# Gated delta rule in one fused decoder layer: the second gate of a unit is projected behind the unit's values

## Chip, cores and metric

The kernel runs on one core of a Trainium2 chip. The metric is device time in microseconds, the median over runs. The engines in the profile are PE (TensorE matmuls; PEld its weight loads), DVE (VectorE), ACT (ScalarE), POOL (GpSimd) and SP (SyncE, which issues DMAs).

## What is computed

One layer of a hybrid decoder on 2048 tokens of width 1024. One input projection feeds four head groups (retention, gated delta rule, S5, GLA), each gated by a SiLU gate; an output projection maps their concatenation back. The change touches the gated delta rule group (4 heads, chunks of 64 tokens):

```python
def _deltanet_branch(qkv, beta_in, a_in, gate, ...):
    qkv = silu(_causal_conv(qkv, conv_w))            # 4 taps, per channel
    q, k, v = split and reshape to heads
    o = _gated_delta_rule(q, k, v, sigmoid(beta_in), g)
    return _merge(_head_rmsnorm(o, norm_g)) * silu(gate)

def _gated_delta_rule(q, k, v, beta, g):             # per chunk of 64
    a_mat = strictly lower part of (kb @ k.T) * decay
    u, w  = solve (I + a_mat) with right sides v*beta and kb*exp(gcum)
    # over the chunks, in order:
    v_new = u - w @ state
    o     = qg @ state + attn @ v_new
    state = state * gl + kg.T @ v_new
```

## The kernel before

The projections are matmuls in split fp16: 24 matmuls of 128x256 (8 slices of the contraction, 3 products of high and low parts) give one 128x256 block. `proj_ops` (line 301 in the trace) projects a tile of 128 tokens, `projT_ops` (line 309) gives 128 channels of a unit of 256 tokens, transposed.

The delta rule is the phase `phase_dn`. It works on 8 units of 256 tokens (two tiles, t = 0 and 1) in a software pipeline: step s of the loop projects and convolves unit s (`conv`), prepares unit s - 1 (`dn_front`, `dn_sub`), and finishes unit s - 2 (`dn_back`). The pieces are:

- `conv(s)`: the dense stream. Keys (dk), queries (dq) and values (dv), two halves of 128 channels each: 24 matmuls of line 309, then ScalarE copies the block out of PSUM (raw, line 1473) and makes the first tap (cva, line 1478), VectorE adds three taps (cva), ScalarE takes a tanh (cvt, line 1484) and VectorE the last product (ckq or cv, line 1488). Between the matmuls `conv` calls `dn_pre` five times: GpSimd builds masked decays (dgx, line 1557), TensorE sums them (line 1568, once per tile), ScalarE exponentiates (dE), GpSimd multiplies by masks (dmb, line 1570); then ScalarE squares keys and queries (dsq, line 1575), TensorE adds up the squares (line 1582), and VectorE makes the norms (depsq, dkk, dry, drt and so on) and scales dmb.
- `dn_front` multiplies keys with keys and queries (line 1627) and scales by dmb. `dn_sub` solves the 16x16 diagonal blocks on VectorE (28 small products dgm and dsV), with the data laid out through DRAM by SyncE's DMAs.
- `dn_back` joins the blocks (lines 1734 to 1776, with the additions dT of line 1755 and copies on ScalarE), forms u and w (lines 1786, 1787), and runs the state through the four chunks. For each chunk TensorE multiplies w with the state (line 1812), VectorE subtracts (VS, line 1813), TensorE makes the next state (line 1818) out of the decays dKG, which GpSimd builds (lines 1804, 1805), and ScalarE copies it (VS, line 1820). Line 1824 gives the outputs of a tile. `finish` squares them (fsq), makes a reciprocal square root on VectorE (fss, fry, frt, frr) and multiplies by the gate.
- The gate of a tile (`gate_ops`): 24 matmuls of line 301, a tanh on ScalarE (th, line 371), and a product on VectorE (dgg, line 375).

`emit` interleaves the streams in proportion: the dense stream, 17 places for `dn_back`, 9 for `dn_front`. Work for other engines is put off by a number of places (`later`, `string`). The order in which an engine gets its instructions then comes from a scheduler of the framework, and each engine works strictly in that order. In steps s = 2 to 7 the dense stream holds both gates of unit s - 2 besides the projections of unit s:

```python
gate = [list(self.gate_ops(..., 2 * u + t, "dgg", ...)) for t in range(2)]
g0, g1 = (0, 104)
dense = dense[:g0] + gate[0] + dense[g0:g1] + gate[1] + dense[g1:]
```

`dense` has 161 places, 52 for the keys, 54 for the queries, 55 for the values; place 104 is the last matmul of the queries' second half. All blocks of these projections share two PSUM buffers (`psA`, tile name pa).

Of the kernel before, what the change touches and what calls it, by code (L numbers as in the profile page):

```python
# [155 lines left out]
class Trunk:  # L156
# [1262 lines left out]
    def phase_dn(self):  # L1419
# [5 lines left out]
        P = self.dP = self.pool("dn", bufs=2, side="right")  # L1425
# [16 lines left out]
        kq, vv, fr, tt, gates = {}, {}, {}, {}, {}  # L1442
# [55 lines left out]
        def sg_ops(i):  # L1498
            return self.gate_ops(P, *self.W["sg"], i, "cva", lambda x: nc.sync.dma_start(self.y[i * 128:(i + 1) * 128, 512:768], x), P1)

        def loads(s, j):
            a, b = {(NU, 0): (1, 0), (NU, 1): (2, 1), (NU, 2): (3, 2), (NU, 3): (0, 3)}.get((s, j), (0, 0))
            ops = [lambda: self.load_b(f"wo{b}")] if b else []
            return ops + [lambda: self.load_a(f"wo{a}")] if a else ops

        def steps(gen, n):

            return [lambda: next(gen, None)] * n

        for s in range(NU + 2):  # L1510
            streams = []
            dense = list(conv(s)) if s < NU else []
            u = s - 2
            if u >= 0:
                gate = [list(self.gate_ops(P, *self.W["dg"], 2 * u + t, "dgg", lambda g, t=t: gates.__setitem__(2 * u + t, g))) for t in range(2)]
                if s < NU:
                    g0, g1 = (0, 104)
                    dense = dense[:g0] + gate[0] + dense[g0:g1] + gate[1] + dense[g1:]
                else:
                    sg = [op for i in (range(10) if s == NU else range(10, NT)) for op in sg_ops(i)]  # L1520
                    n = len(sg) // 3
                    sg = loads(s, 0) + sg[:n] + loads(s, 1) + sg[n:2 * n] + loads(s, 2) + sg[2 * n:] + loads(s, 3)
                    tg = int(len(sg) * 0.717)
                    dense = gate[0] + sg[:tg] + gate[1] + sg[tg:]
                state = [VS]
                streams.append(steps(self.dn_back(u, fr.pop(u), tt.pop(u), state, gates), 16) + [lambda: None])
            u1 = s - 1
            if 0 <= u1 < NU:
                streams.append(steps(self.dn_front(u1, kq[u1], vv[u1], fr[u1], tt), 4) + [lambda: None] * 5)
            if s == NU + 1:  # L1530
                self.out_open()
                self.fronts = {}
                streams.append([op for i in range(2) for op in steps(self.out_front(i, self.out_room[i].__getitem__, self.fronts), 3)])
            self.emit(dense, *streams)
            if u >= 0:
                VS = state[0]
            if s in (3, 5):
                self.load_a("sg" if s == 3 else "wo0")
            if s in (4, 6):
                self.load_b("sg" if s == 4 else "wo0")  # L1540
# [441 lines left out]
```

## Time and profile before

| | us |
|---|---|
| median of 3 runs | 1224.54 (1223.58 to 1227.66) |
| the profiled execution | 1231.87 |
| its span | 1229.8 |
| PE busy in the span | 1116.9 (91%) |
| DVE busy | 911.0 (74%) |
| ACT busy | 505.7 (41%) |
| POOL busy | 471.1 (38%) |
| mean granted TensorE clock | 0.959 |

Durations of single instructions come from the one profiled execution, whose span is the time between its first and last instruction. A row of the trace's timeline gives the start, the length, engine, line, operation and tiles (output <- inputs), and in brackets the idle time of the engine just before and what ended it. Lines with a count group instructions that follow each other.

The steps s = 2 to 7 start at about 658, 706, 752, 801, 846 and 896 us, by the tanh of their first gate, and the last of them hands over about 942 us. Steps 4 and 6 (752 and 846 us) also carry the preparation of one more weight matrix (`load_b`, lines 262 to 265).

### The profile page before, as it was taken

Reading aid. Unit: us, or ns where it says so; the run is one execution under the profiler, and the core shown is the slowest. Engines: PE = TensorE matmul, PEld = TensorE weight load, DVE = VectorE, ACT = ScalarE, POOL = GpSimd, SP = SyncE. Lnnn points to the kernel's source line nnn. Section 1 sums busy time; section 2 is a strip of 40 time slices with the busy share of each in tenths; the row PEclk is TensorE's granted clock in tenths of the full one; section 3 lists DMA queues with packets and bytes.
Section 4 is the critical chain, followed back from the end, with each engine's and each line's share of the span. In section 5 each row is a group of like instructions: output and inputs, shape, how many; then the busy total and the mean of one; then the engine's idle time right before and its main releaser. Section 6 shows DMA issues by size and latency. Waiting matters only on the chain. (4 is left out here: it accounts for less than half of the span.)

```text
span 1229.8 us, 38305 instructions
## 1 busy us (share of the span) xinstructions
PE 1116.9 (91%) x15687; PEld 929.8 (76%) x15687; DVE 911.0 (74%) x3237; ACT 505.7 (41%) x1124; POOL 471.1 (38%) x848
## 2 busy tenths in 40 slices
PE   3889999999999999989779889898899999899996
PEld 2767788888878887877667677677777877788885
DVE  6779655445888788887797877877787744778885
ACT  5733322124444444453454344344443533443431
POOL 3112111111676666563552432533522312444433
PEclk9899999999989999999998998999899989999999
DMA  8565611201121111221212121211123616567652
GB/s 288 146 168 129 173 62 35 70 31 57 26 61 36 36 35 36 65 61 23 88 46 34 28 42 18 61 27 34 30 58 81 181 44 194 140 187 177 183 138 86
DMA packets 186911, 104.97 MB, mean 85 GB/s; under 512 B 158000, under 2 KB 173552, under 8 KB 184560
## 3 DMA queue, kind: packets, MB, share of 16 engines
q1 hardware_dynamic: 186160, 102.00, 32.1%
q8 instruction: 123, 2.02, 0.7%
q10 hardware_dynamic: 576, 0.52, 0.1%
q14 instruction: 52, 0.43, 0.1%
HBM read 59.43 MB, written 26.23 MB: 70 GB/s over the span
## 5 line engine op out<-in xcount | busy, mean ns | idle before, releaser
L301 PEld LDWEIGHTS <-xT 128*128 128x128 f16 x3456 | 337.4, 101 | 78.3 <-issue 22.0
L301 PE MATMUL pa<-w,xT 128*128 128x256 f16 x3072 | 384.4, 280 | 7.4 <-DVE w L265 3.3
L309 PE MATMUL pa<-xT,w 128*128 128x256 f16 x1536 | 202.4, 281 | 8.8 <-ACT raw L1473 7.0
L309 PEld LDWEIGHTS <-w 128*128 128x128 f16 x1536 | 147.7, 101 | 35.6 <-issue 11.1
L1858 PE MATMUL o<-w,yT 128*128 128x256 f16 x1344 | 155.5, 276 | 7.4 <-DMA yT<-y 7.3
L1858 PEld LDWEIGHTS <-yT 128*128 128x128 f16 x1344 | 132.5, 99 | 27.9 <-DMA yT<-y 10.0
L153 DVE SCALAR_TENSOR_TENSOR cva<-raw,cw,cva 128x256 f32<-128x256 f32 x144 | 80.3, 559 | 22.3 <-ACT cva L1478 20.8
L1869 POOL TENSOR_TENSOR ot<-of,npost 128x256 f32<-128x256 f32 x64 | 56.3, 898 | 50.7 <-ACT of L1867 50.7
L153 ACT ACTIVATE gE<-gE 128x384 f32<-128x384 f32 x96 | 45.6, 516 | 56.2 <-DVE gE L153 26.4
L153 DVE TENSOR_REDUCE fss<-fsq 128x4 f32<-128x256 f32 x48 | 19.8, 413 | 56.6 <-ACT fsq L408 56.6
L1472 POOL COPY raw<-raw 128x3 f32<-128x3 f32 x48 | 19.5, 413 | 110.1 <-DVE cva L153 75.1
L301 PE MATMUL pa<-wsu,xT 128*128 128x280 f16 x384 | 52.9, 298 | 7.4 <-DMA xT<-h 3.6
L265 DVE SCALAR_TENSOR_TENSOR w<-stg,wgs,w 128x256 f16<-128x256 f32 x96 | 50.3, 580 | 9.6 <-POOL w L262 9.6
L1147 POOL TENSOR_TENSOR ropq<-ropm,ropn 128x256 f32<-128x256 f32 x16 | 12.8, 797 | 113.4 <-DVE ropn L1144 105.4
L408 ACT ACTIVATE fsq<-o 128x256 f32<-128x256 f32 x48 | 18.2, 379 | 82.1 <-PE o L1195 57.5
L1868 DVE SCALAR_TENSOR_TENSOR ojk<-of 128x256 f32<-128x256 f32 x64 | 40.0, 625 | 14.2 <-ACT of L1867 11.7
L371 ACT ACTIVATE th<-pa,hd 128x256 f32<-128x256 f32 x64 | 30.1, 470 | 42.8 <-PE pa L301 40.4
L1484 ACT ACTIVATE cvt<-cva 128x256 f32<-128x256 f32 x48 | 20.0, 416 | 65.0 <-DVE cva L153 64.8
L1179 POOL TENSOR_TENSOR sg<-sbd,cst 64x128 f32<-64x128 f32 x30 | 12.8, 425 | 80.4 <-DVE sbd L1180 68.8
L1299 PE MATMUL sc<-gE 32*32 32x32 f32 (+1 forms) x2944 | 39.7, 200 | 1.5 <-DVE KK L910 1.5
L1299 PEld LDWEIGHTS sc<-gE 32*32 32x32 f32 (+1 forms) x2944 | 33.8, 105 | 8.8 <-issue 2.1
L1804 POOL TENSOR_TENSOR dKG<-dkh,dkgd 64x256 f32<-64x256 f32 x32 | 21.9, 683 | 47.2 <-PE c L1818 47.2
(420 smaller groups left out, 2329.1 us busy)
## 6 DMA issues: line engine op xcount, KB each, us to landing
x<-in_x SPq DMA_DIRECT2D x16, 512.0 KB, 4.4
stg<-in_wi SPq DMA_DIRECT2D x8, 1024.0 KB, 5.0
yo<-y_d SPq DMA_DIRECT2D x14, 512.0 KB, 4.4
xo<-in_x SPq DMA_DIRECT2D x14, 512.0 KB, 3.6
out<-xo SPq DMA_DIRECT2D x13, 512.0 KB, 3.8
y_d<-fsq SPq DMA_DIRECT2D x48, 128.0 KB, 1.8
xT<-in_wi SPq DMA_DIRECT2D x4, 1024.0 KB, 7.5
rope<-in_rope SPq DMA_DIRECT2D x16, 256.0 KB, 3.0
```

Of the source, the lines that this page charges most:

```text
L153: return lambda *a, **k: self.ops.append(lambda: getattr(self.engine, name)(*a, **k))
L265: nc.vector.scalar_tensor_tensor(dst[:, 1, k, :], st[:, k, :], gs[:, k:k + 1], dst[:, 0, k, :], op0=ALU.mult, op1=ALU.subtract)
L301: yield lambda k=k, i=i, a=a, b=b: self.nc.tensor.matmul(out, xt[:, a, k, t0:t0 + 128], w[:, b, k, :], start=(k == 0 and i == 0), stop=(k ...
L309: yield lambda k=k, i=i, a=a, b=b: self.nc.tensor.matmul(out, w[:, b, k, c0:c0 + 128], xt[:, a, k, :], start=(k == 0 and i == 0), stop=(k ...
L371: nc.scalar.activation(th, ps[0], AF.Tanh, scale=self.half(dsc))
L1299: nc.tensor.matmul(box[0][po:po + pn, e, c0:c0 + rh.shape[1]], lh[r], rh[r], start=True, stop=True, tile_position=(32 * (2 * hp + e), col))
L1472: nc.gpsimd.tensor_copy(x[:, 0:3], x[:, 256:259])
L1484: nc.scalar.activation(th[0], a, AF.Tanh, scale=0.5)
L1804: nc.gpsimd.tensor_tensor(KG[r, c], f["kh"][r, t], f["kgd"][r, t, :].unsqueeze(2).to_broadcast([64, 4, 64]), op=ALU.mult)
L1858: nc.tensor.matmul(o, yT[:, a, k, :], w[:, b, k, :], start=(k == 0 and q == 0 and j % per == 0), stop=(k == 7 and q == 2 and j % per == pe ...
L1868: nc.vector.scalar_tensor_tensor(jk, of[:, cs], 1.0, of[:, cs], op0=ALU.mult, op1=ALU.mult, accum_out=so[:, j:j + 1])
L1869: nc.gpsimd.tensor_tensor(t1[:, cs], of[:, cs], npost[:, cs], op=ALU.mult)
```

## The change

Gate 1 is no longer put ahead of the last matmul of the queries, but behind all of the unit's projections. Its result then arrives when the loop variable has moved on, so the index of the tile is bound when the operation is made.

```diff
             if u >= 0:
-                gate = [list(self.gate_ops(P, *self.W["dg"], 2 * u + t, "dgg", lambda g, t=t: gates.__setitem__(2 * u + t, g))) for t in range(2)]
+                gate = [list(self.gate_ops(P, *self.W["dg"], 2 * u + t, "dgg", lambda g, i=2 * u + t: gates.__setitem__(i, g))) for t in range(2)]
                 if s < NU:
-                    g0, g1 = (0, 104)
-                    dense = dense[:g0] + gate[0] + dense[g0:g1] + gate[1] + dense[g1:]
+                    dense = gate[0] + dense + gate[1]
```

Lines behind the edit have numbers lower by one in the changed kernel. The order of the instructions moves on every engine in steps 2 to 7; three places of step 5 (801 us) follow. The numbers behind a tile's name are buffers.

GpSimd, step 5, behind the decays dKG of the second tile; before:

```order
L1472 COPY raw_1507_10267<-raw_1507_10267 128x3
L1557 TENSOR_TENSOR dgx_14294<-g_709_4199,cst_75 128x512
L1688 MEMSET dsV_14122 64x256
L1570 TENSOR_TENSOR dmb_13664<-dE_13663,cst_75 128x512
L1604 COPY dgl_13858<-dE_13663 128x8
L1690 MEMSET dsV_14122 64x16
L1472 COPY raw_1508_10268<-raw_1508_10268 128x3
L1804 TENSOR_TENSOR dKG_14241<-dkh_13449,dkgd_13100 64x256
```

and with the change:

```order
L1472 COPY raw_1507_10267<-raw_1507_10267 128x3
L1556 TENSOR_TENSOR dgx_14294<-g_709_4199,cst_75 128x512
L1569 TENSOR_TENSOR dmb_13664<-dE_13663,cst_75 128x512
L1603 COPY dgl_13810<-dE_13663 128x8
L1472 COPY raw_1508_10268<-raw_1508_10268 128x3
L1687 MEMSET dsV_14122 64x256
```

On GpSimd itself only the clearing of dsV moves, behind dmb and the copy of raw. What dgx and dmb of the second tile wait for, line 1568 (now 1567) on TensorE, has moved from behind the wait of line 1818 to ahead of line 1811, the state product of the second tile's first chunk.

VectorE, step 5, around the two subtractions VS of the second tile; before:

```order
L153 TENSOR_TENSOR dsV_13388<-dsV_13388,dgm_13392 64x15
L1813 TENSOR_TENSOR VS_13512<-dQ_13503,c_13703 64x256
L153 COPY dsV_13388<-dsV_13388 64x256
L153 SCALAR_TENSOR_TENSOR fry_13714<-frt_13715,fry_13714 128x4
L153 TENSOR_SCALAR frr_13713<-fry_13714,hd_1657_11455 128x4
L153 SCALAR_TENSOR_TENSOR fsq_13777<-o_13637,frr_13713,dgg_13383 128x64 x4
L375 SCALAR_TENSOR_TENSOR dgg_13764<-th_13744,pa_13693 128x256
L1813 TENSOR_TENSOR VS_13512<-dQ_13503,c_13768 64x256
L153 SCALAR_TENSOR_TENSOR cva_13750<-raw_1508_10268,cw_10265,cva_13750 128x256 x3
L1488 SCALAR_TENSOR_TENSOR ckq_13377<-cvt_13813,cva_13750 128x256
L153 TENSOR_REDUCE fss_13867<-fsq_13838 128x4
```

and with the change:

```order
L153 SCALAR_TENSOR_TENSOR cva_13696<-raw_1508_10268,cw_10265,cva_13696 128x256
L153 TENSOR_TENSOR dsV_13388<-dsV_13388,dgm_13392 64x15
L1812 TENSOR_TENSOR VS_13512<-dQ_13503,c_13713 64x256
L153 COPY dsV_13388<-dsV_13388 64x256
L153 SCALAR_TENSOR_TENSOR cva_13696<-raw_1508_10268,cw_10265,cva_13696 128x256
L153 SCALAR_TENSOR_TENSOR frt_13726<-frt_13726 128x4
L153 SCALAR_TENSOR_TENSOR cva_13696<-raw_1508_10268,cw_10265,cva_13696 128x256
L153 SCALAR_TENSOR_TENSOR fry_13725<-frt_13726,fry_13725 128x4
L153 TENSOR_SCALAR frr_13724<-fry_13725,hd_1657_11455 128x4
L153 SCALAR_TENSOR_TENSOR fsq_13782<-o_13637,frr_13724,dgg_13383 128x64
L1488 SCALAR_TENSOR_TENSOR ckq_13377<-cvt_13750,cva_13696 128x256
```

The convolution of the queries' second half stands around the subtractions where it stood behind both; the second subtraction follows two fsq later, and depsq of the norms comes one fsq behind it. The gate's product dgg has left this place for one behind the norms, ahead of the chain fss.

TensorE, step 5, around the sums of squares; before:

```order
L301 MATMUL pa_13898<-w_10381,xT_12_108 128x256
L1582 MATMUL t_13842<-cst_75,dsq_13832 128x2 x8
L1627 MATMUL t_13959<-ckq_13377 64x128
L309 LDWEIGHTS w_10054
L309 MATMUL pa_13752<-xT_13_109,w_10054 128x256
```

and with the change:

```order
L1817 MATMUL c_13820<-VS_13512,dKG_13677 64x64 x4
L301 LDWEIGHTS xT_11_107
L301 MATMUL pa_13852<-w_10381,xT_11_107 128x256
L1581 MATMUL t_13794<-cst_75,dsq_13784 128x2 x8
L1823 MATMUL o_13826<-VS_13512,dST_12595 64x64 x2
```

Before, line 1582 stood behind the outputs of the tile, 24 matmuls of the values and 8 of the next step's gate 0; now it follows one gate matmul behind line 1817, and between the wait for the first subtraction and it stand 7 value and 6 gate matmuls.

## Rows read from the trace of the kernel before

**Rows 1.** Busy time by stretch: stretch, its length, busy us per engine, granted clock, DMA

```profile
801.00:846.00 45.00, 40.71 (x680) 32.62 (x677) 36.10 (x124) 19.97 (x44) 17.93 (x30) 0.97 0.18 33
```

**Rows 2.** TensorE's waits, 656 to 942 us: total us, times, longest us

```profile
PE c L1818 <- DVE VS L1813: 6.3, 4, 2.0
PE c L1818 <- DVE frr L153: 5.0, 2, 2.5
PE c L1818 <- DVE fry L153: 2.1, 1, 2.1
```

**Rows 3.** Timeline of TensorE, step at 801 us

```profile
822.19 1.59 PE L301 MATMUL pa<-w,xT 128*128 128x256 f16 x13
825.75 0.65 PE L1818 MATMUL c<-VS,dKG 128*64 128x64 f32 x8 [1.96 <-DVE VS L1813]
...
833.47 1.95 PE L1582 MATMUL t<-cst,dsq 128*128 128x2 f32 x16 [0.34 <-ACT dsq L1575]
...
835.71 2.79 PE L309 MATMUL pa<-xT,w 128*128 128x256 f16 x24
```

**Rows 4.** Busy time around three waits; columns as in rows 1

```profile
776.70:780.30 3.60, 3.60 (x23) 2.64 (x24) 1.28 (x5) 1.72 (x5) 0.88 (x3) 0.53 0.36 76
...
871.00:879.30 8.30, 8.30 (x64) 6.23 (x65) 3.76 (x9) 2.46 (x6) 3.74 (x7) 0.59 0.50 88
823.80:825.80 2.00, 0.05 (x1) 0.08 (x2) 1.97 (x15) 0.00 (x0) 0.00 (x0) 1.00 0.00 0
825.80:833.40 7.60, 7.33 (x81) 5.96 (x81) 6.16 (x15) 4.32 (x10) 5.18 (x9) 1.00 0.61 105
```

**Rows 5.** Timeline of VectorE: subtraction, depsq and dT; two links

```profile
728.83 0.41 DVE L1813 TENSOR_TENSOR VS<-dQ,c 64x256 f32<-64x256 f32 x1
...
749.83 1.22 DVE L1755 TENSOR_TENSOR dT<-dT,l 32x128 f32<-32x128 f32 x4
...
775.36 0.16 DVE L153 TENSOR_TENSOR frt<-fry 128x4 f32<-128x4 f32 x1
775.56 0.16 DVE L153 SCALAR_TENSOR_TENSOR frt<-frt,fss 128x4 f32<-128x4 f32 x1
...
825.19 0.41 DVE L1813 TENSOR_TENSOR VS<-dQ,c 64x256 f32<-64x256 f32 x1
...
835.45 0.17 DVE L153 TENSOR_SCALAR depsq<-t 128x8 f32<-128x8 f32 x1 [0.21 <-PE t L1582]
...
843.87 1.23 DVE L1755 TENSOR_TENSOR dT<-dT,l 32x128 f32<-32x128 f32 x4 [0.15 <-PE l L1751]
...
917.73 0.41 DVE L1813 TENSOR_TENSOR VS<-dQ,c 64x256 f32<-64x256 f32 x1
...
936.08 1.22 DVE L1755 TENSOR_TENSOR dT<-dT,l 32x128 f32<-32x128 f32 x4
```

**Rows 6.** Timeline of GpSimd: decays of the first and second tile

```profile
720.80 1.04 POOL L1557 TENSOR_TENSOR dgx<-g,cst 128x512 f16<-128x512 f16 x1 [1.99 <-PE t L1568]
721.80 1.64 POOL L1570 TENSOR_TENSOR dmb<-dE,cst 128x512 f32<-128x512 f32 x1
...
823.03 0.18 POOL L1472 COPY raw<-raw 128x3 f32<-128x3 f32 x1
827.57 1.04 POOL L1557 TENSOR_TENSOR dgx<-g,cst 128x512 f16<-128x512 f16 x1 [4.36 <-PE t L1568]
...
828.83 1.26 POOL L1570 TENSOR_TENSOR dmb<-dE,cst 128x512 f32<-128x512 f32 x1
```

**Rows 7.** Timeline of VectorE beside the first pair of rows 6

```profile
720.61 0.22 DVE L153 TENSOR_TENSOR dsV<-dsV,dgm 64x63 f32<-64x63 f32 x1
720.86 1.06 DVE L153 TENSOR_TENSOR dgm<-dsV 64x60 f32<-64x60 f32 x1
721.84 0.47 DVE L153 SCALAR_TENSOR_TENSOR cva<-raw,cw,cva 128x256 f32<-128x256 f32 x1
722.24 1.28 DVE L153 TENSOR_TENSOR dsV<-dsV,dgm 64x60 f32<-64x60 f32 x1
```

**Rows 8.** Timeline of ScalarE, the squares in the step at 801 us

```profile
832.36 1.06 ACT L1575 ACTIVATE dsq<-ckq 128x1024 f32<-128x1024 f32 x1
```

## The prediction, made before the changed kernel ran

> **What bounds the kernel now.** The change touches six steps of one loop, s = 2 to 7, which lie in the trace between 658 and 942 us; everything else keeps its order. I read the trace from coarse to fine: the busy time of a step, what TensorE waits for in these steps, one step's instructions in order of time, and then VectorE and GpSimd around the longest wait.
>
> A step takes 45 to 50 us. In the step from 801 to 846 us TensorE is busy 40.7 of 45.0 us and VectorE 36.1 [rows 1], so neither is full: the step is a chain that changes engines. In the list of TensorE's waits one consumer stands out. The matmul of line 1818 (state times decay) waits for VectorE, 6.3 us over four waits, 5.0 over two and 2.1 once [rows 2]. Its releaser is named VS, frr or fry, but these are neighbours in one queue: it needs the subtraction VS of line 1813. In the step at 801 us TensorE has issued its cover (13 gate matmuls), is done by 823.8, and waits 1.96 us [rows 3].
>
> VectorE is busy 1.97 of the 2.00 us of that wait [rows 4]: the small products of the triangular solve (dgm, dsV), the convolution (cva) and the links of a reciprocal square root are in line ahead of it. So **its arrival there is a term of the step's length**. From it one can walk to the next point where all engines meet, the four additions dT (line 1755) that release line 1766 and with it the next step's keys: from the subtraction's end, 825.19 + 0.41 = 825.60, to the start of dT, 843.87, it is 18.3 us in this step, 20.6 us in the step at 706 us and 17.9 us in the last one [rows 5].
>
> **What makes VectorE late.** GpSimd. With nothing on GpSimd a dsV product of the solve takes 0.22 us; the next one (dgm), started 0.06 us after a dgx product of GpSimd, takes 1.06 and ends 0.08 us after it, and one that meets a dmb product takes 1.28 us [rows 6, 7]. Against 0.22 they lose 0.84 and 1.06 us, 1.90 together; that dmb itself took 1.64 us where another takes 1.26 [rows 6]. One of the two engines waits each time.
>
> The Trainium skill (SBUF — State Buffer, section "SBUF: two separate sides") says that a VectorE instruction with two SBUF inputs and a GpSimd instruction that reads SBUF exclude each other for a whole instruction. By that rule the pair dgx and dmb would cost VectorE its full 1.04 + 1.26 = 2.30 us, where the rows give 1.90; the total below would be 2 us higher.
>
> **The change, part by part.** Nothing is added or removed: 24 matmuls, a tanh, a product of gate 1 per step stand elsewhere. Three moves matter.
>
> (a) *Ahead of the subtraction.* Without gate 1 in their way, the last matmul of the queries and the product of line 1568 for the second tile are issued ahead of the state product instead of after its wait. So a cva (0.47 us, [rows 7]) now stands ahead of the subtraction. And GpSimd's second dgx and dmb, which in this profile wait 4.36 us for line 1568 and run from 827.57 on, after the subtraction, are free to run when GpSimd has finished the four dKG and a small copy, at 823.2 [rows 6]: just in the 2 us in which VectorE works through small products towards the subtraction. Price 0.47 + 1.90 = 2.4 us. Bounds: 0.5, if VectorE gets through first; 2.8, if both block in full.
>
> (b) *From the subtraction to depsq.* TensorE has there line 1818 (0.65), 7 matmuls at 2.79/24 = 0.116 us, line 1812 (about as 1818), the second subtraction, 6 gate matmuls, 1818 again, and then at once line 1582 (1.95) [rows 3]. That is 0.65 + 0.8 + 0.65 + 0.7 + 0.65 + 1.95 = 5.4 us; with some 0.8 us for the copy of the state, queued on ScalarE behind the tanh of the queries, 6.2. The square dsq (1.06 us, [rows 8]) fits in beside it, so its wait (0.34 us here) goes. Before it was 835.45 - 825.60 = 9.85 us [rows 5], with gate 1's remainder, 24 value matmuls and gate 0 in between. Gain 3.65 us.
>
> (c) *From depsq to dT.* 8.4 us before [rows 5]. The normalisation chain of the second tile, half done by depsq before, now stands wholly behind it: about eight more links at 0.2 us from start to start [rows 5] and gate 1's product (0.4), less four products fsq of about 0.2 that now come after dT, and some 0.7 for links that no longer run laced with another chain. Price 1.9 us.
>
> Values and gate 1 now fill TensorE's end of the step in place of the values alone; that covers work that is on no wait, and I cost it at nothing. Should it fail, line 1766 waits for dT instead, which is the third rival.
>
> (d) *The clock.* The wait at line 1818 grows from 1.96 to some 4.4 us. The two waits of 2.5 us [rows 2], which end at 776.7 and 871.0, were followed by a granted clock of 0.53 and 0.59 over 3.6 and 8.3 us, that is mostly the 1.2 GHz level; the one of 1.96 was followed by 1.00, 2.4 GHz [rows 4]. So I expect the lower level behind the longer wait, and there it falls on (b), whose 5.4 us are TensorE's. It loses 1.8 us (half of 3.6) to 3.3 (most of (b)); I take 2.4.
>
> **The sum.** Step at 801 us: 2.4 - 3.65 + 1.9 + 2.4 = +3.0. Step at 706: two more links ahead of the subtraction (0.35), and (b) + (c) = 6.2 + 10.3 = 16.5 us take the place of 20.6, part of which was a stretch at the low clock: 2.75 - 4.1 + 2.4 = +1.0. Step at 896: no dgx is left, so 1.5 ahead, 16.5 for 17.9, and half a clock term for a wait of 3 us: +1.3. The steps at 752 and 846 also carry eight weight products of a load: their low clock is there already, the gain of (b) is used up by (c) and by the loads' ScalarE halves, which now queue behind the solve's first copy; I take (a) alone, +2.4 each. In the first step (658) the pair moves ahead of one wait of line 1818 and away from another: 0. Together **+10.1 us**.
>
> The trace is of one execution of 1231.87 us with a span of 1229.8; it lies 7 us above the median of the three runs, 1224.54. The difference carries over: 1242 in its terms, **1234.6 us** for the runs, 0.8% slower.
>
> **Rivals.** *Faster: the hole is closed.* The subtraction is served before the pair blocks it and the clock holds. For: TensorE's order has no gap left between the values and line 1582, and dsq's wait goes. Then (a) is 0.5 and (d) nothing: -1.25 at 801, -3.3 at 706, -0.9 at 896, -1.25 for each loaded step: -8, 1216.5 us. It turns on whether GpSimd is free by 823; in this trace it is [rows 6].
>
> *No change.* The blocking comes, the clock holds: +0.6, -1.4, +0.1 and twice +0.6: under 1 us, 1225. For: the wait of 1.96 us did not bring the clock down [rows 4]. Against: the new wait is over twice that.
>
> *Much slower: a second wait.* TensorE reaches line 1766 early, waits for dT some 1 to 3 us, and the clock falls again, now on the 24 key matmuls (2.8 us at full clock) for whose convolution VectorE sits idle. At the 1.2 GHz level they cost 2.8 us more, in five steps 14: 1248.5. It decides from about 2.5 us of wait on.
>
> **Chances.** Forecast 0.50, second wait 0.11, no change 0.17, faster 0.22. A measurement of this kernel can tell about 0.3% (3.7 us) from no change. So faster 0.22, same 0.17, slower 0.61. The forecast alone, with (a) and (d) between their bounds, is 1228 to 1240. The range, 1216 to 1247, takes in the faster case below and part of the way to the second wait above.
>
> **What would show it.** In the changed profile: GpSimd's second dgx and dmb of a step ahead of the first subtraction of line 1812 (lines behind the edit are one lower), its neighbours on VectorE at about 1 us where they took 0.2; the wait at line 1817 from 2 to over 4 us; then a granted clock near 0.5; line 1581 about 6 us after the subtraction at full clock and 8 to 9 at half; no wait for dsq. I am wrong if that wait stays at 2 us, if the steps get shorter than 45 us, or if the clock stays at 1.00 through them.

## The result, and the profile after

The changed kernel takes 1257.3 us (median of 4 runs, 1256.7 to 1258.9), the kernel before 1225.1 in the same comparison: a ratio of 1.026 (95% interval 1.022 to 1.030), 32 us slower. The forecast was +10 us with a range up to 1247: the sign was right, the size was not.

The profiled execution took 1257.33 us, its span is 1255.5. The loss lies where the change is. From the first addition dT of the step at 706 us to the one that ends the step at 896 us, five whole steps, the kernel before takes 232.5 us and the changed one 260.7. The windows view of this stretch, before (the stretch, its length, busy us of PE, PEld, DVE, ACT and POOL, granted clock, DMA share, GB/s):

```profile
703.56:936.08 232.52, 210.62 (x3371) 168.00 (x3370) 186.65 (x640) 100.23 (x231) 89.44 (x146) 0.95 0.20 39
940.70:1229.80 289.10, 267.12 (x2678) 226.84 (x2675) 199.91 (x651) 113.45 (x244) 97.50 (x116) 0.96 0.53 147
```

and after:

```profile
706.11:966.83 260.72, 230.17 (x3375) 183.14 (x3373) 191.98 (x635) 100.88 (x232) 90.97 (x146) 0.85 0.18 34
970.40:1255.50 285.10, 263.97 (x2679) 224.91 (x2676) 200.59 (x653) 113.68 (x244) 98.10 (x116) 0.97 0.54 150
```

The five steps are 28.2 us longer; the first one (from 668.65 to 703.56 us, now 668.02 to 706.11) is 3.2 longer. Behind the loop the changed execution happens to be shorter (4.0 us in the second row of each, 5.1 from the last dT on), which is why the two spans differ by 25.7 only, while the medians of all runs differ by 32: the profiled execution of the kernel before lies 7 us above its median. The work is the same (3371 and 3375 matmuls); the granted clock fell from 0.95 to 0.85, and TensorE's busy time rose with it.

TensorE's waits from 656 to 972 us (what waited, for whom, total us, times, longest), which answer to [rows 2]:

```profile
PE c L1817 <- DVE VS L1812: 22.5, 6, 4.4
PE l L1765 <- DVE dT L1754: 4.2, 5, 1.4
```

The wait at line 1817 now stands in every step, at 4.2 to 4.4 us in four of them and 2.5 to 2.6 in the first and the last. The other wait that was feared, at line 1765, stayed short.

Step 5, which began at 801 us and now begins at 815, shows the whole mechanism. First VectorE: dT of the step before, the longest product ahead of the subtraction, the subtraction, the norms' depsq, and this step's dT:

```profile
812.17 0.27 DVE L1754 TENSOR_TENSOR dT<-dT,l 32x128 f32<-32x128 f32 x1
835.89 2.96 DVE L153 TENSOR_TENSOR dgm<-dsV 64x55 f32<-64x55 f32 x1
841.16 0.41 DVE L1812 TENSOR_TENSOR VS<-dQ,c 64x256 f32<-64x256 f32 x1
849.83 0.17 DVE L153 TENSOR_SCALAR depsq<-t 128x8 f32<-128x8 f32 x1 [3.60 <-PE t L1581]
861.86 0.27 DVE L1754 TENSOR_TENSOR dT<-dT,l 32x128 f32<-32x128 f32 x1
```

GpSimd beside that product:

```profile
835.63 0.80 POOL L1804 TENSOR_TENSOR dKG<-cst,dgl 64x256 f32<-64x256 f32 x1
836.39 0.18 POOL L1472 COPY raw<-raw 128x3 f32<-128x3 f32 x1
836.53 1.03 POOL L1556 TENSOR_TENSOR dgx<-g,cst 128x512 f16<-128x512 f16 x1
837.53 1.25 POOL L1569 TENSOR_TENSOR dmb<-dE,cst 128x512 f32<-128x512 f32 x1
```

The product dgm of 64x55 elements started at 835.89, under the last dKG, and ended at 838.85, 0.07 us after dmb: dgx and dmb passed in between, and VectorE stood still for both. They are now ahead of the subtraction, where in [rows 6] they came behind it. The other steps show the same meeting: one product of 2.95 us in the steps at 709 and 864 us, two of 1.01 and 1.20 us in the step at 760 and, beside a dmb alone, one of 1.21 us in the last.

Then TensorE:

```profile
835.76 1.59 PE L309 MATMUL pa<-xT,w 128*128 128x256 f16 x13
841.72 1.08 PE L1817 MATMUL c<-VS,dKG 128*64 128x64 f32 x8 [4.36 <-DVE VS L1812]
842.74 1.67 PE L309 MATMUL pa<-xT,w 128*128 128x256 f16 x7
844.34 1.11 PE L1811 MATMUL c<-VS,dW 64*64 64x64 f32 x8
845.39 1.46 PE L301 MATMUL pa<-w,xT 128*128 128x256 f16 x6
...
847.83 0.28 PE L301 MATMUL pa<-w,xT 128*128 128x256 f16 x1
847.95 1.84 PE L1581 MATMUL t<-cst,dsq 128*128 128x2 f32 x16
...
849.99 1.70 PE L309 MATMUL pa<-xT,w 128*128 128x256 f16 x14
...
852.12 1.27 PE L309 MATMUL pa<-xT,w 128*128 128x256 f16 x10
853.23 2.02 PE L301 MATMUL pa<-w,xT 128*128 128x256 f16 x17
...
855.94 1.26 PE L301 MATMUL pa<-w,xT 128*128 128x256 f16 x10
857.14 0.69 PE L1733 MATMUL l<-dT,dLT 32*32 32x16 f32 x60
...
859.50 0.69 PE L1745 MATMUL l<-dQ,dT 32*32 32x16 f32 x62 [1.12 <-ACT dQ L1736]
```

and the same stretch before (the rows that [rows 3] left out):

```profile
826.33 0.61 PE L301 MATMUL pa<-w,xT 128*128 128x256 f16 x4
826.78 0.27 PE L309 MATMUL pa<-xT,w 128*128 128x256 f16 x1
...
828.28 1.92 PE L309 MATMUL pa<-xT,w 128*128 128x256 f16 x16
...
831.21 1.05 PE L309 MATMUL pa<-xT,w 128*128 128x256 f16 x8
832.10 1.04 PE L301 MATMUL pa<-w,xT 128*128 128x256 f16 x8
...
839.19 0.69 PE L1734 MATMUL l<-dT,dLT 32*32 32x16 f32 x60
```

Count the projections' and gates' 128x256 matmuls between the subtraction and the matmuls of line 1733 (1734 before), on which dT rests. Before: 37 (4, 1, 16, 8, 8) up to the norms of line 1582, then 24: 61, and the four of line 1568 besides. After: 14 (7, 6, 1) up to the norms, then 51 (14, 10, 17, 10): 65. **The norms have moved forward, the work ahead of dT has hardly become less.** Over the five steps it is 295 such matmuls, 299 before. So in step 5 depsq comes 8.3 us behind the subtraction instead of 9.9, and dT comes 12.0 us behind depsq instead of 8.4.

The clock, in the stretches behind the long waits of the steps at 709, 760, 815, 864 and 920 us (columns as in the windows above):

```profile
734.70:749.00 14.30, 14.30 (x86) 11.00 (x87) 6.62 (x29) 4.24 (x9) 4.01 (x9) 0.52 0.32 52
786.60:800.00 13.40, 13.39 (x75) 10.26 (x75) 6.43 (x21) 3.88 (x9) 3.43 (x8) 0.50 0.32 53
841.70:848.00 6.30, 6.28 (x40) 4.57 (x40) 3.09 (x12) 2.17 (x5) 0.49 (x2) 0.51 0.53 84
891.10:906.00 14.90, 14.86 (x86) 11.57 (x87) 6.71 (x29) 4.30 (x9) 3.88 (x10) 0.50 0.30 50
945.30:957.00 11.70, 11.40 (x69) 9.49 (x69) 7.64 (x28) 4.23 (x9) 3.19 (x6) 0.56 0.41 69
```

Behind each wait TensorE works almost without a gap at or near the 1.2 GHz level, in three of five steps for 13 to 15 us. The same five steps from the end of the subtraction to the end of line 1734 (1733), summed by the windows view; before, then after:

```profile
sum 78.15, PE 74.47 PEld 60.75 DVE 60.01 ACT 37.39 POOL 47.77; mean PE 14.89 PEld 12.15 DVE 12.00 ACT 7.48 POOL 9.55
sum 91.72, PE 90.69 PEld 72.73 DVE 54.46 ACT 29.23 POOL 39.58; mean PE 18.14 PEld 14.55 DVE 10.89 ACT 5.85 POOL 7.92
```

With the change TensorE is busy for 90.69 of 91.72 us here, with about as many matmuls as before, at a granted clock of 0.64, 0.64, 0.81, 0.62 and 0.72 where it was 0.80, 0.89, 1.00, 0.80 and 1.00. The stretch is 13.6 us longer; from line 1733 to dT it is 3.1 us more.

### The profile page after: what moved, and what is told of

Read it like the earlier page. It is cut to its first block, busy times and chain, and to the rows that moved or that the text cites. A ratio compares the mean times of both kernels' runs of the same rounds, so it can differ in the third digit from the quotient of the medians.

```text
span 1255.5 us, 38294 instructions
## 1 busy us (share of the span) xinstructions
PE 1134.1 (90%) x15687; PEld 942.9 (75%) x15687; DVE 916.9 (73%) x3237; ACT 505.9 (40%) x1124; POOL 473.2 (38%) x848
## 4 chain that ended last, share of the span: by engine, by line
DVE 21%; PE 21%; ACT 3%; issue 3%; DMA 1%; POOL 1%; DVEq 0%; ACTq 0%; POOLq 0%; SPq 0%
PE pa L309 5%; PE pa L301 5%; DVE cva L153 2%; DVE ojk L1867 2%; DVE dgm L153 2%; DVE dsV L153 2%; PE o L1857 2%; PE t L1581 2%; PE c L1817 1%; DVE ort L153 1%; DVE y L1069 1%; DVE xo L1878 1%; PE c L1811 1%; DVE w L265 1%; DVE ory L153 1%
## 5 line engine op out<-in xcount | busy, mean ns | idle before, releaser
L309 PE MATMUL pa<-xT,w 128*128 128x256 f16 x1536 | 211.2, 288 | 9.6 <-ACT raw L1473 8.5
L309 PEld LDWEIGHTS <-w 128*128 128x128 f16 x1536 | 150.4, 103 | 38.8 <-issue 10.2
L1147 POOL TENSOR_TENSOR ropq<-ropm,ropn 128x256 f32<-128x256 f32 x16 | 12.5, 780 | 113.3 <-DVE ropn L1144 105.0
L371 ACT ACTIVATE th<-pa,hd 128x256 f32<-128x256 f32 x64 | 30.2, 471 | 46.9 <-PE pa L301 44.6
L1867 DVE SCALAR_TENSOR_TENSOR ojk<-of 128x256 f32<-128x256 f32 x64 | 40.6, 634 | 10.5 <-ACT of L1866 8.0
L1817 PE MATMUL c<-VS,dKG 128*64 128x64 f32 x248 | 25.6, 257 | 24.4 <-DVE VS L1812 22.5
L1817 PEld LDWEIGHTS c<-VS,dKG 128*64 128x64 f32 x248 | 20.8, 164 | 32.4 <-issue 29.0
```

What stands on the lines that cost most here:

```text
L309: yield lambda k=k, i=i, a=a, b=b: self.nc.tensor.matmul(out, w[:, b, k, c0:c0 + 128], xt[:, a, k, :], start=(k == 0 and i == 0), stop=(k ...
L371: nc.scalar.activation(th, ps[0], AF.Tanh, scale=self.half(dsc))
L1817: nc.tensor.matmul(pS[r, h, :], KG[:, c, h, :], VS[:, c, h, :], start=True, stop=True)
L1867: nc.vector.scalar_tensor_tensor(jk, of[:, cs], 1.0, of[:, cs], op0=ALU.mult, op1=ALU.mult, accum_out=so[:, j:j + 1])
```

## The experiments

Three theories, which the expectations name. **A, the clock:** VectorE is blocked, the wait grows, and what costs is the low clock behind it. **B, the order:** gate 1 behind the values costs by its place on TensorE, whatever the clock does. **C, the queues:** VectorE and ScalarE, each in its own order, set the time of dT, and TensorE's speed matters little.

For each run the five steps are split at the same three points as in the prediction: from dT to the end of the subtraction (the term (a)), from there to depsq (b), from depsq to the next dT (c); the clock's term (d) falls into these. The table gives sums over the five steps, of the starts of these rows in each run's timeline, with the clock of the same five steps; "decays" is where line 1567 of the second tile, and so GpSimd's dgx and dmb, stands. The sums come from one profiled execution each: late_decay's is the shortest of its six (1232.1 us, the median is 1241.9), early_decay's the longest of its four (1253.5, 1247.9), and the kernel before's lies 7 us above its median. The first step is not in these sums: it takes 34.9 us before and 38.1 with the change, 39.6 in early_decay, 41.7 in early_fill_20, 38.3 in after_q and 42.2 in fill_after_q.

| run | gate 1 | decays | ratio to before (95%) | (a) | (b) | (c) | five steps | clock |
|---|---|---|---|---|---|---|---|---|
| before | old | behind the wait | 1 | 132.7 | 55.2 | 44.6 | 232.5 | 0.95 |
| the change | new | ahead of it | 1.026 (1.022 to 1.030) | 144.2 | 45.2 | 71.3 | 260.7 | 0.85 |
| late_decay | new | behind | 1.012 (1.008 to 1.016) | 131.6 | 31.5 | 78.8 | 241.9 | 0.92 |
| early_decay | old | ahead | 1.017 (1.014 to 1.020) | 143.9 | 63.3 | 44.3 | 251.5 | 0.89 |
| decays_ahead_after | new | far ahead | 1.013 (1.010 to 1.016) | 143.1 | 33.9 | 69.1 | 246.1 | 0.93 |
| decays_ahead_before | old | far ahead | 1.009 (1.006 to 1.011) | 143.2 | 54.8 | 44.6 | 242.6 | 0.93 |
| early_fill | old | ahead, filled 36 | 1.022 (1.019 to 1.025) | 144.3 | 63.6 | 44.4 | 252.2 | 0.95 |
| early_fill_20 | old | ahead, filled 20 | 1.009 (1.006 to 1.012) | 142.9 | 54.2 | 44.5 | 241.6 | 0.96 |
| fill_after | new | ahead, filled 36 | 1.029 (1.024 to 1.034) | 148.3 | 41.3 | 81.7 | 271.4 | 0.90 |
| fill_after_v | new | ahead, filled 36 | 1.024 (1.019 to 1.029) | 143.4 | 32.2 | 84.2 | 259.8 | 0.91 |
| after_q | new | ahead | 1.020 (1.015 to 1.024) | 143.5 | 46.0 | 67.7 | 257.2 | 0.87 |
| fill_after_q | new | ahead, filled 36 | 1.015 (1.010 to 1.019) | 142.0 | 43.0 | 66.1 | 251.0 | 0.93 |
| late_order_fill | new | behind, filled 20 | 1.016 (1.013 to 1.020) | 136.5 | 36.6 | 79.2 | 252.3 | 0.91 |
| fill_before | old | behind, filled 18 | 0.993 (0.991 to 0.995) | 131.3 | 51.0 | 47.0 | 229.2 | 0.96 |
| fill_before_24 | old | behind, filled 24 | 0.996 (0.994 to 0.998) | 132.1 | 51.6 | 44.3 | 227.9 | 0.99 |
| cover_before | old | see below | 1.000 (0.997 to 1.003) | 135.9 | 42.9 | 48.1 | 226.9 | 0.95 |

### The two parts of the change apart

The change moves gate 1, and with it line 1567 of the second tile. In late_decay the gate is moved and the decays are put back; in early_decay only the decays are moved. The places at which `conv` calls `dn_pre` do it, 118 in place of 96 in the changed kernel and 92 in the kernel before:

```diff
-                        if pos in (48, 88, 96, 124, 128):
+                        if pos in (48, 88, 118, 124, 128):
```

> The change stays; only line 1567 of the second tile (and with it GpSimd's dgx and dmb) goes back behind the wait of line 1817. Theory A (clock): the blocked VectorE makes the wait over 4 us, the wait brings the clock down, and the low clock costs nearly all of the 32 us. Then here the wait is about 2 us, the time at the low level falls from some 85 us in steps 2 to 7 to under 40, and the time is 1225 to 1238 us. Theory B (order): 24 gate matmuls now stand between the norms and dT, and that order alone costs the time whatever the clock does: 1250 to 1258 us.

Measured: 1241.9 us (1232.1 to 1249.0), between the bands of A and B.

> The kernel before; only line 1568 of the second tile is put ahead of line 1812, as the change has it, and gate 1 stays where it was. Theory A (clock): GpSimd blocks VectorE, the wait of line 1818 grows from 2 to about 4 us, the clock falls behind it, 1240 to 1255 us. Theory B (order): the blocking alone costs at most the 2 us of each of five steps, and gate 1 still stands ahead of the norms: 1225 to 1235 us.

Measured: 1247.9 us (1246.0 to 1253.5), inside A's band. With gate 1 untouched, the moved decays alone cost 1.7% of the 2.6%. Both verdicts stand in each run's list of TensorE's waits (700 to 965 us). early_decay:

```profile
PE c L1818 <- DVE VS L1813: 18.7, 9, 4.6
```

late_decay, in which the hole is 3.1 us at most, and another wait has come up:

```profile
PE c L1817 <- DVE VS L1812: 12.1, 5, 3.1
PE l L1745 <- ACT dQ L1736: 6.6, 3, 3.1
```

So blocking and order both cost. In the table they even stand in different columns: (a) is 142 to 148 wherever the decays run ahead of the subtraction and 131 to 137 where they don't; (c) is 44 to 48 with gate 1 in its old place and 66 or more in its new one. But (b) falls where (c) rises, so the order's price is in their sum: 99.8 us before, 110.3 in late_decay.

### The decays far ahead

Here line 1567 stands among the queries' first matmuls, so that the pair should be done before the last products of the solve (`pos in (48, 62, 68, 124, 128)` in both kernels).

> The changed kernel with both calls of line 1567 some 27 places earlier (among the queries' first matmuls), so that GpSimd's dgx and dmb are done before the last products of the solve run ahead of the subtraction. Theory A: the wait of line 1817 is 2 to 2.6 us instead of 4.4, the low level shrinks from 85 to under 55 us in steps 2 to 7, 1230 to 1243 us. Theory B: 1250 to 1258 us.

> The kernel before with line 1568 moved in the same way, gate 1 in its old place. Theory A: a wait of line 1818 of under 2 us and fewer low stretches, 1215 to 1225 us. If the pair's blocking costs nothing where it stands before: 1223 to 1229 us.

Measured: 1238.2 us (1233.4 to 1239.9), inside A's band; and 1233.2 us (1232.3 to 1233.9), over both bands. Moving the pair away from the wait didn't take its price away: term (a) is 143 in both, 10.5 us above the kernel before. In decays_ahead_after the waits of line 1817 are shorter but more, nine where the changed kernel has five long ones in the five steps:

```profile
PE c L1817 <- DVE VS L1812: 17.5, 9, 2.6
```

What VectorE loses to the pair on its way to the subtraction it loses at either place (in the five stretches of (a) it is busy for 116.8 us in decays_ahead_before, for 105.7 in the kernel before); only behind the subtraction does it cost less. Between the two runs, with blocking and clock alike (143.1 and 143.2, 0.93 and 0.93), only the gate's place is left, and this is the cleanest pair on it: **3.5 us lost in five steps, made of 20.9 gained in (b) and 24.5 lost in (c)** (5.0 us by the medians of the whole runs). The clock is alike over the five steps, not in each stretch: between the subtraction and dT, decays_ahead_before spends 20.6 us at the low level and decays_ahead_after 12.5, so the gate's place costs more than 3.5 rather than less. The forecast had a gain there, 1.75 us in the step at 801, 4.1 at 706, 1.4 at 896 and none in the other two: 7.25 us.

### Filling the hole

To part the clock from the wait, the hole is filled with matmuls whose result nobody reads. VectorE's lateness is left as it is.

```diff
+    def fill(self, s, n):
+        out = self.ps("l")[:, 0:256]
+        for k in range(n):
+            self.nc.tensor.matmul(out, self.W["dv"][0][:, 0, k % 8, 0:128], self.xT[s][:, 0, k % 8, :], start=True, stop=True)
...
                 if c == 0 or i + 1 < NT:
+                    if t == 1 and c == 0 and u + 2 < NT // 2:
+                        self.fill(u + 2, 36)
                     pS = ps4("c")
```

> The change stays; in the hole ahead of line 1817 (second tile, first chunk) TensorE gets 36 more matmuls of 128x256 a step, of work that nobody reads, into a free PSUM buffer (36 times 0.116 us is 4.2 us). VectorE and GpSimd are left as they are, so the subtraction is as late as before. Theory A (clock): no idle time, the clock stays at 1.00, and the time falls by 20 to 30 us, to 1227 to 1237. Theory B (order): no change, 1252 to 1260; a filling that only gets in the way would make it slower still.

> The kernel before with line 1568 of the second tile early (as in early_decay, 1247.9 us) and 36 matmuls of unread work a step ahead of line 1818, in the hole that the blocked VectorE leaves there (4.3 to 4.9 us). GpSimd and VectorE meet as in early_decay. Theory A (the price is the clock that falls behind the wait): the clock holds, 1225 to 1235 us. Rival (the price is the time that VectorE loses itself, or the order): 1243 to 1252 us.

Measured: 1263.6 us (1256.1 to 1272.0) and 1248.7 us (1246.6 to 1251.6). The first lies over both bands, the second in that of A's rival. But the fillings had moved more than they should: with them the scheduler put other instructions ahead. In fill_after ScalarE's square dsq and the copies dF went ahead of the copy of the state:

```profile
PE c L1816 <- ACT VS L1826: 10.6, 4, 2.8
```

and in early_fill line 1739 (1734 before) went ahead of the norms, where it waits for a transfer:

```profile
PE l L1739 <- DMA dT<-ttd: 9.8, 5, 2.9
```

A hole was filled and another opened. Neither run tells the theories apart. Next the copy of the state was put on VectorE in the filled change (`nc.vector.tensor_copy(dst, pS[r])` for the second tile's first chunk):

> The changed kernel with the 36 matmuls of unread work as in fill_after, and with the copy of the state behind line 1817 (second tile, first chunk) on VectorE, so that it doesn't queue behind dsq and dF on ScalarE, where a new wait of 2.6 us came up in fill_after. Theory A (clock): 1228 to 1240 us. Theory B (24 gate matmuls between the norms and dT cost by their place): 1250 to 1265 us.

Measured: 1249.8 us (1247.2 to 1261.0), just under B's band. The norms now come early, (b) is 32.2, and dT comes as much later, (c) is 84.2. But the second state product had slipped behind 17 matmuls of gate and values, so the order was again not the change's own.

Two fillings keep the order nearly (between the norms and line 1733 fill_after_q has 44 of the 128x256 matmuls in each step, the change 44 to 52; early_fill_20 has 24, as early_decay). For the filled change dsq was made to wait for the copy of the state, through a scale of one that GpSimd makes out of it; after_q has that wait alone. For early_decay 20 matmuls are few enough.

```diff
                     nc.scalar.activation(dst, pS[r], AF.Copy)
+                    if t == 1 and c == 0 and u + 2 < NT // 2:
+                        self.one = self.t(P, [128, 1], "one")
+                        nc.gpsimd.memset(self.one[64:128], 1.0)
+                        nc.gpsimd.tensor_scalar(self.one[0:64], VS[0:64, 1, 0, 0:1], 0.0, 1.0, op0=ALU.mult, op1=ALU.add)
...
-        nc.scalar.activation(sq.rearrange("p s j t -> p (s j t)"), kq.rearrange("p s j t -> p (s j t)"), AF.Square)
+        nc.scalar.activation(sq.rearrange("p s j t -> p (s j t)"), kq.rearrange("p s j t -> p (s j t)"), AF.Square, scale=self.one if u >= 2 else 1.0)
```

> The changed kernel with 36 matmuls of unread work a step in the hole ahead of line 1817, and with dsq (ScalarE) made to wait for the copy of the state, so that ScalarE and TensorE keep the changed kernel's order, which the two fillings before did not. Theory A (clock): the hole has no idle time, the clock holds, and the stretch from the subtraction to dT, in which TensorE is busy at the low level in the changed kernel, shrinks by 3 to 5 us a step: 1228 to 1240 us. Theory C (VectorE's and ScalarE's queues set dT whatever TensorE does): that stretch stays, 1250 to 1262 us.

> The control for it: the changed kernel with dsq made to wait in the same way, and nothing filled. Both theories: as the changed kernel, 1254 to 1260 us, with waits of over 4 us at line 1817.

> As early_fill, with 20 matmuls a step (2.3 us of the hole of 4.3 to 4.9), which leaves line 1739 where early_decay has it, so that the new wait for a transfer does not come. Theory A (clock): idle time of about 2 us is left, fewer low stretches than early_decay (67.7 us at the low level from 650 to 950), 1233 to 1241 us. Theory C: 1243 to 1252 us.

Measured: fill_after_q 1242.3 us (1241.4 to 1247.4), between the bands; after_q 1250.7 us (1247.0 to 1256.4), a little under its band; early_fill_20 1235.0 us (1232.3 to 1241.2), inside A's band. **Here the clock has its price:** early_decay loses 19.0 us in five steps, early_fill_20 9.1, at a clock of 0.96 instead of 0.89 and with the subtraction as late as before (142.9 and 143.9). Of the 9.9 us that the filling gives back 9.1 lie in (b), 63.3 to 54.2, where TensorE works at the low level: between the subtraction and dT the time at that level falls from 44.0 to 20.5 us. By the medians, each against the kernel before beside it, 21.0 us of loss become 9.9. The 9.1 left in the five steps are term (a), 10.2 over the kernel before. In the changed kernel the filling of 36 gives 6.2 us in the five steps (257.2 in after_q to 251.0) and 8.4 by the medians, though the first step gets 3.9 longer, and the new order keeps its 66 us in (c). It brought a new wait of its own:

```profile
PE c L1816 <- ACT VS L1826: 6.3, 5, 1.7
```

These waits add up to 6.3 us over the five steps, so the filling may have taken up to 6.2 + 6.3 = 12.5 us off the clock's price there. That need not be all of it: between the subtraction and dT, 30.7 us at the low level are left, of 49.1 in after_q.

### The order alone

> The changed kernel with line 1567 of the second tile put back behind the wait (as late_decay), with 20 matmuls of unread work in the hole, and dsq behind the copy of the state (as fill_after_q): no blocking, no idle hole; of the change only the place of gate 1 is left, with the norms 5 to 6 matmuls of 128x256 behind the second state product in place of 37 in the kernel before. If the prediction's gain behind the subtraction is real (3.65 less 1.9 a step): under the kernel before with its hole filled (1218.6 us), 1208 to 1216. If TensorE's work from line 1817 to line 1745 (some 66 such matmuls in both orders) sets dT and the norms' place gives nothing: 1217 to 1226 us. If the new order costs 2 us a step, as the filled change suggested: 1227 to 1236 us.

Edit: late_decay's places, 20 matmuls filled, dsq behind the copy of the state. Measured: 1244.2 us (1240.0 to 1248.3), above all three bands, with the forecast's gain farthest off. It isn't the order alone either: waits for the copy of the state (5.6 us) and for dQ (7.2) are in it, and the clock is 0.91. What it shares with the other runs with the new order is that the norms come early, (b) 36.6, and dT late, (c) 79.2.

Where dT is lost is best read in late_decay. Its ScalarE, step 3:

```profile
740.64 0.46 ACT L371 ACTIVATE th<-pa,hd 128x256 f32<-128x256 f32 x1
744.58 0.42 ACT L1484 ACTIVATE cvt<-cva 128x256 f32<-128x256 f32 x1 [3.48 <-DVE cva L153]
744.90 0.37 ACT L408 ACTIVATE fsq<-o 128x256 f32<-128x256 f32 x1
745.16 0.36 ACT L1736 ACTIVATE dQ<-l,cst 128x128 f32<-128x128 f32 x1
```

and the kernel before, step 5:

```profile
840.00 0.51 ACT L1478 ACTIVATE cva<-raw,cw 128x256 f32<-128x256 f32 x1
840.42 0.35 ACT L1737 ACTIVATE dQ<-l,cst 128x128 f32<-128x128 f32 x1
842.21 0.42 ACT L1484 ACTIVATE cvt<-cva 128x256 f32<-128x256 f32 x1 [1.45 <-DVE cva L153]
```

With line 1733 later on TensorE, the copy dQ, which it feeds, stands behind the tanh cvt of the values' second half. That tanh waits 3.48 us for VectorE's convolution, and dQ, line 1745 and dT wait with it. That is theory C's part: from the end of line 1733 to dQ, the five steps lose 13.3 us in late_decay and 11.5 in decays_ahead_after, against 3.6 before. The changed kernel has this order too (in step 5 cvt starts at 858.50 and dQ at 859.08), but loses only 4.1 there, since the low clock makes line 1733 late as well: the two delays lie beside each other, which may be why taking one of them away gave so little.

### What gains

> The kernel before with 18 such matmuls (2.1 us) a step ahead of line 1818, in its hole of 1.4 to 2.5 us. Theory A (clock): the low stretches behind the waits of 2.5 us at 776 and 871 us go (3.4 and 6.8 us at the low level, and what they drag behind them): 1215 to 1222 us. Theory B: no change, 1223 to 1228 us.

> The kernel before with 24 matmuls of unread work a step in place of 18 (2.8 us, over the hole of 2.0 to 2.5). If the clock is what fill_before gained by: the same or a little better, 1214 to 1221 us. If the matmuls get in the way once they are longer than the hole: 1220 to 1226 us.

Measured: fill_before 1218.6 us (1217.1 to 1221.6), inside A's band; fill_before_24 1220.2 us (1217.6 to 1222.9), at the upper end of its first band. **Matmuls that nobody reads make the kernel before 0.7% faster** (0.4% with 24). The long waits of line 1818 are gone (the longest left are 1.1 and 1.6 us), and the five steps take 229.2 and 227.9 us. This beats both kernels. Where it is all gained is not shown: with the first step the loop is 2.3 and 3.4 us shorter in the profiled executions, against 8.2 and 5.2 by the medians, and 24 matmuls cut the time at the low level in the six steps from 27.3 to 6.8 us without gaining more than 18, which left 20.5.

> The kernel before with line 1818 (second tile, first chunk) put one place of its stream later, behind four more gate matmuls and line 1568: work of the kernel itself in the hole, in place of the unread matmuls of fill_before (1218.6 us). Theory A: 1216 to 1226 us if the hole gets shorter; but line 1568 now stands ahead of the wait, and where GpSimd then blocks VectorE as in early_decay it is 1235 to 1250 us.

Edit: one more `yield` ahead of line 1818 (second tile, first chunk), and no empty place at the end of the stream. Measured: 1224.7 us (1216.6 to 1231.5), inside A's band but no change. Its holes are still 1.0 to 1.9 us, and GpSimd's second pair runs ahead of the subtraction in one of the five steps only. These five are the shortest of the table, but the first step is 4.0 us longer than before, and ten runs spread over 15 us; the kernel's own work didn't do what the unread matmuls did.

## Why the prediction was wrong in size

Term by term, over the five steps:

- **(a), ahead of the subtraction: right in its mechanism.** Forecast 2.75 + 2.4 + 2.4 + 2.4 + 1.5 = 11.45 us; measured 144.2 - 132.7 = 11.5. That the sums meet so closely is partly luck: by step it is 2.7, 2.0, 1.2, 2.2 and 3.4, and the last contains 6.8 us at the low level where the kernel before had none. The order, the pair of GpSimd and the 4.4 us of waiting came as written. The dgm that met the pair took 2.96 us instead of the 0.62 of the same product before, 2.34 more. The Trainium skill (SBUF — State Buffer, section "SBUF: two separate sides") lets VectorE lose the pair whole; dgx and dmb took 1.03 + 1.25 = 2.28 us, so here the trace agrees with it, and the 1.90 from [rows 7] was a little low. early_decay and early_fill_20 show the term without the gate: 11.2 and 10.2.
- **(b) to (c), from the subtraction to dT: wrong, and this is the step that failed.** Forecast -4.1, 0, -1.75, 0 and -1.4 for the order, with the clock's +6.0 together -1.25 us; measured +16.7, of which (b) is -10.0 and (c) +26.7. (b) itself was near: 8.26 us in step 5 where 8 to 9 were given for the low clock, and 20.9 us in five steps, 4.2 a step, between the two runs with the decays far ahead. (c) was put at +1.9 in step 5 and is +3.6 there, +5.3 a step on average. The sentence that failed is "that covers work that is on no wait, and I cost it at nothing". The matmuls taken out from ahead of the norms don't vanish: they now stand between the norms and line 1733, in the same queue, and dT needs line 1733. 51 matmuls instead of 24 at 2.79/24 us are 3.1 us more, of the 3.57 by which line 1733 ends later behind depsq in step 5 (8.00 against 4.43). Over the five steps line 1733 ends 23.5 us later behind depsq (46.5 against 23.0), nearly all of the 26.7; 115 more matmuls there (235 for 120) are 13.4 us of it at full clock. I followed VectorE's links from depsq to dT; the path ran over TensorE.
- **In the loaded steps** (752 and 846 us) I took the loss in (c) for used up by the gain in (b). It is 7.1 and 6.4 us there, against gains of 2.2 and 3.0.
- **(d), the clock: right in mechanism, but mis-sized, the second step that failed.** It was priced at 6.0 us for three steps and denied to the loaded ones. Behind the waits of over 4 us the low level lasted 6 to 15 us in all of them. Between the subtraction and dT the changed kernel spent 58.9 us at the low level, the kernel before 17.2. From early_decay to early_fill_20, 23.5 us less of it made this stretch 8.9 us shorter, 0.38 us for each; at that rate the 41.7 us more are 16 us (an estimate). It fits the 13.6 us by which TensorE takes longer for about as many matmuls up to line 1733.
- **The first step** was put at 0 and lost 3.2 us: there too the wait came (2.6 us).

11.5 + 16.7 + 3.2 is 31.4 us, of a measured 32. How the 16.7 divide is settled by estimates only: some 14 to 16 us for the clock, which leaves 1 to 3 for the order, where a gain of 7.25 was forecast. With the decays out of the way the order costs more: 3.5 by the pair with the decays far ahead and 10.5 by late_decay against the kernel before (110.3 for 99.8 us behind the subtraction, at a clock of 0.92 for 0.95). The two overlap, and no run held the changed kernel's clock without moving something else.

The rivals: "faster" fell because GpSimd was free in time; "no change" because the clock did not hold and the order gained nothing; "a second wait" at line 1765 stayed at 1.4 us and was not the reason, though its time was the nearest. The first two were priced with a gain of 1.75 us behind the subtraction in each loaded step, where the forecast had none.

## What to carry to other kernels

A result that comes earlier gains nothing if the next meeting point waits for other work in the same queue: before an edit is credited, count the instructions of each engine from one meeting point to the next, on all engines, in both orders. Moving one instruction moves what hangs on it on the other engines too, here two GpSimd products, whose move alone costs 1.7% of the 2.6%. Where a short, regular wait brings the clock down and the engine is the bound behind it, unread matmuls in the hole can pay.

## What was not expected of the hardware

The low clock outlasted the wait by far: from 786.6 to 800.0 us TensorE was busy for 13.39 of 13.40 us and was granted 0.50 throughout. A wait of 4.20 us stood ahead of it, while a wait of 4.36 us at 841.7 was followed by 6.3 us of it. So a wait's length did not set how long the level stayed low: 2.46 us brought 0.56 over 11.7 us. A wait of 1.96 us left the clock at 1.00 in the kernel before [rows 4].
